# Four matmuls with a combined query weight in place of six, in the cached-key scores of the sample group

## The chip, the cores and the metric

The kernel runs on one core of one Trainium2 chip. A core has five engines that run their own instruction queues in order: PE (TensorE, matrix products into PSUM banks), DVE (VectorE), ACT (ScalarE), POOL (GpSimd) and SP (SyncE, which here issues most DMA transfers). They wait for each other through semaphores only. The time of a kernel is the device time of one execution in microseconds (us), given as the median of several runs. Beside the times there is one profiled execution, whose records (busy time of each engine, waits, the chain of work that ended last, the clock granted to PE) are quoted below.

## What is computed

The program is one step of a decoder layer for two groups of tokens that share all weights: a prompt of 1024 tokens and a sample group of 8 sequences with 8 new tokens each (64 tokens, in all 1088 columns). A layer has two token mixers side by side (sparse attention with an indexer that picks 256 keys per query, and gated linear attention), an output projection, a layer norm, a squared-ReLU MLP with 4096 hidden channels and a second layer norm.

The change is in the sparse attention of the sample group. For each of the 8 sequences, 8 queries by 8 heads (64 rows) are compared with 4096 keys of a paged cache and with the new keys; keys that were not picked are masked; softmax and the product with the values follow. Cut to that:

```python
s = jnp.einsum('bqkgd,bqskd->bqkgs', qg, k_sel).astype(jnp.float32) * (HEAD_DIM ** -0.5)
s = jnp.where(valid[:, :, None, None, :], s, -jnp.inf)
p = jax.nn.softmax(s, axis=-1).astype(v_sel.dtype)
o = jnp.einsum('bqkgs,bqskd->bqkgd', p, v_sel)
```

The kernel doesn't gather the picked keys: it scores all 4096 cached keys and adds a mask of large negative numbers.

Every fp32 number that enters a matmul is split into a high part (rounded to the type `fp32r`) and a low part (the remainder). A product x·y is then formed as three matmuls: high·high, high·low and low·high, which add up in one PSUM bank.

## The kernel before, in words

The program has two parts. `front` makes all projections, the indexer, the prompt's attention and the gated linear attention; it is not touched, and its instructions are the same in both kernels. `back` holds the MLP, and inside it, as work that is dealt in between, the sample group's attention on its cache.

**Who sets the order.** The program is unrolled when it is built. A planner (`Clock`, `Stream`, `Order`) holds a list of Python generators, the streams. Each yields what its next step needs, as tiles that must be ready or as a condition. The planner keeps an estimated time for each engine (`Clock.note`, fed by `Clock.cost`), and always takes the first stream of the list whose needs are met by the time of PE; `slack` says by how much DVE and ACT may be booked ahead of PE and the stream still be stepped. So the order of each engine's queue is fixed when the program is built. On the chip each engine takes its queue in that order.

**The filler.** `main` (through `feed`, `ff1_unit`, `ff2_unit`) is the MLP for column blocks 0 and 1 (384 columns each), in groups of four hidden blocks. One unit of the first layer is 24 matmuls of 384 columns into a bank named `pf1`, one of the second is 12 matmuls into `pf2` (the profile calls both `pf`). It is the last stream in the list and is stepped whenever nothing else may be. A unit's result goes through ACT and DVE (`fr`), ACT (`a`) and DVE or POOL (the low part of `a`).

**The scores.** `at_scores` works on four pairs of sequences p, eight chunks of 512 keys each. A chunk n is loaded by eight DMAs on SP (`k_load`, tile `ckr`), split by ACT (`ckh`, high) and DVE or POOL (`ckl`, low) in `k_split`, and multiplied with the queries `aqz` into a bank `psc`. The queries of a pair lie as the 128 columns of a weight: 64 columns for sequence 0 of the pair, 64 for sequence 1. There are four such weights in `aqz`, of 128 columns each: for either sequence the high part and the low part, with zeros in the other sequence's 64 columns, so that both sequences' scores add up in one bank (rows 0 to 63 and 64 to 127):

```python
pe.matmul(ps[:, :n], qz[:, b2, 0], kh, start=first, stop=False)
pe.matmul(ps[:, :n], qz[:, b2, 0], kl, start=False, stop=False)
pe.matmul(ps[:, :n], qz[:, b2, 1], kh, start=False, stop=b2 == 1)
```

One DVE instruction then adds the mask (`msk`, `asn` for the new keys), writes the scores to SBUF (`as`, `ast` for the new keys) and keeps the row's maximum (`amx`). At the start of each pair `at_scores` loads `aq`, clears `aqz` on POOL and fills it by eight small casts on DVE. There is one `aqz`.

**The values.** `at_values` transposes the weights of the softmax (`pst`, `ptl`), multiplies them with the cached values (`cv`, banks `pob`), and at a pair's end divides, transposes back (`sa`, `pso`) and collects (`tall`).

**The merge.** `merge` waits for all four pairs, then multiplies the sample group's columns (block 2, 320 columns) with the attention output weights (`pma`, eight weights `wao`) and the output projection (`pwo`, eight weights `wout`). Its weights come through `Weights V`: raw tiles `vr` (tag `rw`, six buffers, shared with the MLP's raw weights `wr`), split into `v`. After its layer norm the MLP for block 2 runs to the end, followed by the last layer norm.

Of the kernel before, what the change touches and what calls it, by code (L numbers as in the profile page):

```python
# [12 lines left out]
F32 = mybir.dt.float32  # L13
F32R = mybir.dt.float32r
# [3 lines left out]
AF = mybir.ActivationFunctionType  # L18
# [5 lines left out]
P = 128  # L24
# [67 lines left out]
def f32(ap):  # L92
    return ap.bitcast(F32)
# [1902 lines left out]
def back(ph, tc, env, A, O):  # L1996
# [20 lines left out]
    def own(name, shape, dt=F32, bufs=1):  # L2017
        return clock.take(pgs.tile(shape, dt, name=name, tag=name, bufs=bufs), name, "own " + name, bufs)
# [20 lines left out]
    class Weights:  # L2039
# [10 lines left out]
        def load(self):  # L2050
            i = self.split + len(self.raw)
            src, kt = self.src[i]
            rs = []
            if self is W and 3 <= i < 6:
                r = wide(f"{self.name}r{i}", F32, [P, 8, P])[:, :kt]
                sp.dma_start(r, src)
                rs = [r[:, k:k + 4] for k in range(0, kt, 4)]
            for k in range(0, 0 if rs else kt, 4):
                r = clock.take(pgs.tile([P, 4, P], F32, name=f"{self.name}r{i}_{k}", tag="rw", bufs=NRW), f"{self.name}r{i}_{k}", "brw", NRW)
# [316 lines left out]

    def at_scores():
# [6 lines left out]
        for p in range(4):  # L2384

            aq = own("aq", [P, 8, 16], F32R)
            sp.dma_start(f32(aq), f32(env["qa_s"][:, :, TP + 16 * p:TP + 16 * p + 16].rearrange("h p q -> p h q")))
            qz = own("aqz", [P, 512], F32R)
            q6 = qz.rearrange("p (b e c h q) -> p b e c h q", b=2, e=2, c=2, h=8)
            qz = qz.rearrange("p (b e x) -> p b e x", b=2, e=2)  # L2390
            pool.memset(f32(qz), 0.0)
            yield [aq]
            for g in range(2):
                for e in range(2):
                    for par in range(2):
                        r = ((par + e) % 2) * 64
                        x = q6[g * 64:g * 64 + 64, 0, e, 0, 4 * g + par:4 * g + par + 3:2, :]
                        x = view(x, 0, [x.ap[0], [256 + 64, 2], x.ap[1], x.ap[2]])
                        dve.tensor_copy(x, f32(aq[r:r + 64, 4 * g + par:4 * g + par + 3:2]).rearrange("p h (b q) -> p b h q", b=2))
                yield ()  # L2400
# [7 lines left out]
            def scores(ps, n, kb, k0, mcol):  # L2408
                first = True
                for b2 in range(2):  # L2410
                    kh, kl = kb[b2]
                    if n == 512:
                        kh, kl = (x.rearrange("p (i j r) -> p j i r", i=4, j=4) for x in (kh, kl))
# [3 lines left out]
                    first = False  # L2417
                i = k0 // 1024
                so, si = S[i][:, k0 - 1024 * i:k0 - 1024 * i + n], ps[:, :n]
                m = mn if n < 512 else mks[4 * p + i][:, k0 - 1024 * i:k0 - 1024 * i + n]  # L2420
                dve.tensor_tensor_reduce(out=so, in0=si, in1=m, scale=1.0, scalar=NEG, op0=OP.add, op1=OP.max,
                                         accum_out=mx[:, mcol:mcol + 1])
            for qq in range(4):
                yield lambda: len(used) >= 4 * (p - 1) + qq
                S[qq] = xpage(f"as{p}{qq}", F32, [P, 1024])
                for e in range(2):
# [7 lines left out]
                    ps = bank("psc")  # L2434
                    scores(ps, 512, [(h[:, b2], l[:, b2]) for b2 in range(2)], qq * 1024 + e * 512, qq * 2 + e)
# [3 lines left out]
            ps = bank("psc")  # L2439
            scores(ps, TS, [(ka_n[:, 0], ka_n[:, 1])] * 2, PAST, 8)  # L2440
# [11 lines left out]
            blocks.append(S)  # L2452

# [78 lines left out]
    def merge():  # L2532
        yield lambda: "samples" in flags
# [7 lines left out]
        V.load(), V.load()  # L2541
# [13 lines left out]
        for f in range(8):  # L2555
            yield V.landed(1 if f else 2)
            w = V.get(f, 1, 1)
# [11 lines left out]
        yield from outputs(2, lambda f: V.get(8 + f, 1, 2), wide)  # L2569
# [150 lines left out]
    order.add(at_values(), margin=M_VA)  # L2720
    order.add(at_scores(), margin=M_SC)
# [84 lines left out]
```

## Time and profile before

| | before |
|---|---|
| time, median of 3 runs | 2037.97 us (2036.68 to 2038.39) |
| the profiled execution, its own time | 2039.02 us |
| its span, first to last instruction | 2037.3 us |
| mean clock granted to PE | 0.996 of full speed |
| PE, matmuls busy | 2012.7 us, 99% |
| DVE, ACT, POOL busy | 60%, 55%, 38% |
| first and last matmul of the scores (`psc`) | 1190.6 and 1486.2 us |
| matmuls of the merge (`pma`, `pwo`) | 1610.7 to 1717.7 us |

All numbers below are of the span's clock: 0 is the first instruction of the profiled execution. A row of the view of groups names the engine, the operation, the output tile, the input tiles, the shapes, the count, the busy time and the mean duration of one. All instructions have the line L263, since a helper records them; they are told apart by their tiles. The durations that the profile gives for single matmuls overlap each other, so the cost of a matmul to PE is read from a run of them (start of the first to start of the next work) divided by their number.

### The profile page before, as it was taken

How to read it: one execution, taken by the hardware profiler on the slowest of the kernel's cores; microseconds unless marked ns; L12 is line 12 of the kernel's file. 1: busy time of each engine (PE TensorE's matmuls, PEld its weight loads, DVE VectorE, ACT ScalarE, POOL GpSimd, SP SyncE). 2: the span in 40 equal slices, each digit the busy share in tenths (PEclk: the TensorE clock that was granted, in tenths of full speed). 3: DMA queues.
4: the chain of work that ended last, by engine and by line, in shares of the span. 5: the costliest groups of instructions: out<-in, count | busy, mean ns of one | idle time of the engine just before them, and what ended most of it. 6: DMA issues, size and time to landing. Idle time of an engine off the chain costs nothing.

```text
span 2037.3 us, 34522 instructions
## 1 busy us (share of the span) xinstructions
PE 2012.7 (99%) x12439; PEld 1949.4 (96%) x12439; DVE 1227.1 (60%) x2597; ACT 1114.6 (55%) x2217; POOL 775.4 (38%) x582
## 2 busy tenths in 40 slices
PE   9999999999999999999999999999999999999998
PEld 8999999999999999999999999998999999999998
DVE  8897767785655866641366445566554445466635
ACT  6687788897778566650124344544443232445543
POOL 5144232232311131222133335565654343354455
PEclk9999999999999999999999999999999999999998
DMA  9465212212132342364661245554523443145552
GB/s 329 182 211 155 99 35 71 80 54 85 41 115 71 95 144 71 100 221 141 216 222 52 65 121 167 163 166 136 156 90 103 141 132 100 52 141 163 185 151 91
DMA packets 185164, 260.32 MB, mean 128 GB/s; under 512 B 22160, under 2 KB 121488, under 8 KB 184992
## 3 DMA queue, kind: packets, MB, share of 16 engines
q1 hardware_dynamic: 177440, 232.67, 36.0%
q0 software_dynamic: 7552, 25.43, 4.2%
q8 instruction: 98, 1.61, 0.3%
q14 instruction: 74, 0.61, 0.1%
HBM read 208.52 MB, written 49.51 MB: 127 GB/s over the span
## 4 chain that ended last, share of the span: by engine, by line
PE 53%; issue 2%; ACT 1%; DVE 1%; POOL 1%; SPq 0%; DMA 0%; ACTq 0%; POOLq 0%; DVEq 0%
PE pf L263 34%; PE pwo L263 5%; PE pmb L263 4%; PE gate L263 2%; PE pma L263 2%; PE psc L263 2%; PE pob L263 1%; PE pst L263 1%; SPq L263 0%; PE pov L263 0%; ACT pp L263 0%; PE ppt L263 0%; POOL w L263 0%; POOL wl L263 0%; ACT as L263 0%
## 5 line engine op out<-in xcount | busy, mean ns | idle before, releaser
L263 PE MATMUL pf<-a,w 128*128 128x384 f32 (+1 forms) x2304 | 398.3, 330 | 1.5 <-POOL a L263 0.6
L263 PE MATMUL pf<-h,w 128*128 128x384 f32 (+1 forms) x2304 | 394.3, 329 | 0.0
L263 PEld LDWEIGHTS pf<-a,w 128*128 128x128 f32 x2304 | 379.6, 188 | 5.4 <-POOL a L263 0.9
L263 PEld LDWEIGHTS pf<-h,w 128*128 128x128 f32 x2304 | 380.2, 188 | 1.9
L263 POOL TENSOR_TENSOR wl<-wr,wh 128x1024 fp32r<-128x1024 f32 (+1 forms) x67 | 152.9, 2287 | 420.4 <-ACT wh L263 324.7
L263 POOL TENSOR_TENSOR w<-wr,w 128x512 fp32r<-128x512 f32 x135 | 191.1, 1423 | 124.9 <-ACT w L263 114.5
L263 ACT ACTIVATE w<-wr 128x512 fp32r<-128x512 f32 x256 | 147.6, 618 | 39.0 <-PE pf L263 25.9
L263 DVE TENSOR_TENSOR w<-wr,w 128x512 fp32r<-128x512 f32 x121 | 126.8, 1053 | 55.8 <-ACT w L263 54.4
L263 DVE TENSOR_TENSOR acc<-acc,pf 128x384 f32<-128x384 f32 (+1 forms) x152 | 81.4, 539 | 104.9 <-PE pf L263 104.7
L263 POOL TENSOR_TENSOR a<-fr,a 128x384 fp32r<-128x384 f32 (+1 forms) x56 | 54.6, 976 | 199.5 <-ACT a L263 197.1
L263 PE MATMUL gate<-xh,wh 128*128 128x384 f32 (+1 forms) x384 | 129.0, 336 | 0.0
L263 PE MATMUL gate<-xh,wl 128*128 128x384 f32 (+1 forms) x384 | 125.7, 327 | 0.0
L263 PE MATMUL gate<-xl,wh 128*128 128x384 f32 (+1 forms) x384 | 125.6, 327 | 0.0
L263 ACT ACTIVATE wh<-wr 128x1024 fp32r<-128x1024 f32 (+1 forms) x76 | 75.3, 998 | 85.3 <-PE pmb L263 65.9
L263 ACT ACTIVATE fr<-pf 128x384 f32<-128x384 f32 (+1 forms) x96 | 44.9, 467 | 122.9 <-PE pf L263 122.0
L263 DVE TENSOR_TENSOR fr<-fr,pf 128x384 f32<-128x384 f32 (+1 forms) x96 | 50.8, 529 | 95.2 <-ACT fr L263 94.8
L263 ACT ACTIVATE a<-fr 128x384 fp32r<-128x384 f32 (+1 forms) x96 | 48.7, 508 | 77.5 <-DVE fr L263 77.5
L263 DVE TENSOR_SCALAR_CACHE_REDUCE jk<-sc,ga_f 128x1024 int8<-128x1024 f32 (+2 forms) x96 | 88.2, 919 | 1.7
L263 ACT ACTIVATE jkb<-sc,gb_f 128x896 int8<-128x896 f32 (+2 forms) x96 | 86.1, 897 | 5.6 <-DVE gb_f L263 3.2
L263 PE MATMUL psv<-wh,xh 128*128 128x256 f32 x288 | 80.8, 285 | 0.0
L263 PE MATMUL psv<-wl,xh 128*128 128x256 f32 x288 | 80.4, 283 | 0.0
L263 DVE CUSTOM_DVE_ANT_0 pp<-psq,msk 128x512 f32<-128x512 f32 (+3 forms) x96 | 51.4, 554 | 46.2 <-PE psq L263 44.1
(525 smaller groups left out, 5149.9 us busy)
## 6 DMA issues: line engine op xcount, KB each, us to landing
wr<-wff SPq DMA_DIRECT2D x254, 256.0 KB
wr<-w SPq DMA_DIRECT2D x42, 512.0 KB
ckr<-kT SPq DMA_DIRECT2D x256, 64.0 KB
ga_s<-gate SPq DMA_DIRECT2D x16, 544.0 KB
ci_s<-cig SPq DMA_DIRECT2D x16, 512.0 KB
kir<-ci_s SPq DMA_DIRECT2D x16, 512.0 KB
mgp<-ga_s SPq DMA_DIRECT2D x16, 384.0 KB
qa_s<-qa SPq DMA_DIRECT2D x8, 544.0 KB
```

The source lines that it names most:

```text
L263: r = f(*a, **k)
```

## The change

The queries' high part and low part now lie side by side in one weight of 128 columns, one weight for each sequence of a pair: 64 columns high, 64 columns low (for the second sequence the other way round). Each of the two parts of the keys is multiplied with it, into a bank of its own for each sequence. So a chunk takes four matmuls instead of six, and half of a bank holds the scores from the high part of the queries, the other half those from the low part (with low·low, which was left out before). The halves are added afterwards: ACT copies one half (64 rows) to SBUF, DVE adds the other half from PSUM, and the instruction with mask and maximum then reads and writes SBUF. This tail is a stream of its own (`fin`), placed first in the planner's list.

The queries are made by a stream of their own, `at_queries`, with two buffers of `aqz` (256 columns each), from the beginning of the pair before. The streams `at_values` and `at_scores` get `slack=8.0` instead of 2.0. The raw weights of the merge (`Weights V`) are taken into the three buffers of `msk` where one is free in the planner's count, the first two are loaded once the scores are done (flag `scored`), and more raw tiles may be held (3 and 4 instead of 1 and 2).

```diff
-                                  ("aq", [P, 8, 16], F32R, 1), ("aqz", [P, 512], F32R, 1), ("ast", [P, TS], F32, 2), ("amx", [P, 9], F32, 2),
+                                  ("aq", [P, 8, 16], F32R, 1), ("aqz", [P, 256], F32R, 2), ("ast", [P, TS], F32, 2), ("amx", [P, 9], F32, 2),
...
+                if self is V and clock.free.get("own msk", [0]):
+                    r = clock.take(pgs.tile([P, 4, P], F32, name=f"{self.name}r{i}_{k}", tag="msk", bufs=3), f"{self.name}r{i}_{k}", "own msk", 3)
+                else:
+                    r = clock.take(pgs.tile([P, 4, P], F32, name=f"{self.name}r{i}_{k}", tag="rw", bufs=NRW), f"{self.name}r{i}_{k}", "brw", NRW)
...
+    def at_queries():
+        yield lambda: "start" in flags
+        for p in range(4):
+            yield lambda: pair[0] >= p - 1
+            aq = own("aq", [P, 8, 16], F32R)
+            sp.dma_start(f32(aq), f32(env["qa_s"][:, :, TP + 16 * p:TP + 16 * p + 16].rearrange("h p q -> p h q")))
+            t = own("aqz", [P, 256], F32R, bufs=2)
+            pool.memset(f32(t), 0.0)
+            qz = t.rearrange("p (b x) -> p b x", b=2)
+            q5 = t.rearrange("p (c h q) -> p c h q", c=4, h=8)
+            yield [aq]
+            for g in range(2):
+                for e in range(2):
+                    for par in range(2):
+                        r = ((par + e) % 2) * 64
+                        x = q5[g * 64:g * 64 + 64, e, 4 * g + par:4 * g + par + 3:2, :]
+                        x = view(x, 0, [x.ap[0], [64 if e else 192, 2], x.ap[1], x.ap[2]])
+                        dve.tensor_copy(x, f32(aq[r:r + 64, 4 * g + par:4 * g + par + 3:2]).rearrange("p h (b q) -> p b h q", b=2))
+                yield ()
+            qzs[p] = qz
...
-                    pe.matmul(ps[:, :n], qz[:, b2, 0], kh, start=first, stop=False)
-                    pe.matmul(ps[:, :n], qz[:, b2, 0], kl, start=False, stop=False)
-                    pe.matmul(ps[:, :n], qz[:, b2, 1], kh, start=False, stop=b2 == 1)
...
+                ps = [bank(f"psc{b2}", True) for b2 in range(2)]
                 for b2 in range(2):
+                    for e in range(2):
+                        k = kb[b2][e]
...
+                        pe.matmul(ps[b2][:, :n], qz[:, b2], k, start=e == 0, stop=e == 1)
...
-                dve.tensor_tensor_reduce(out=so, in0=si, in1=m, scale=1.0, scalar=NEG, op0=OP.add, op1=OP.max,
-                                         accum_out=mx[:, mcol:mcol + 1])
+                def fin():
+                    for b2 in range(2):
+                        yield [ps[b2][:, :n]]
+                        act.activation(so[64 * b2:64 * b2 + 64], ps[b2][64 - 64 * b2:128 - 64 * b2, :n], AF.Copy)
+                    for b2 in range(2):
+                        x = so[64 * b2:64 * b2 + 64]
+                        yield [x]
+                        dve.tensor_tensor(x, ps[b2][64 * b2:64 * b2 + 64, :n], x, op=OP.add)
+                        unpin(ps[b2])
+                    dve.tensor_tensor_reduce(out=so, in0=so, in1=m, scale=1.0, scalar=NEG, op0=OP.add, op1=OP.max,
+                                             accum_out=mx[:, mcol:mcol + 1])
+                    summed.append(0)
+                order.add(fin(), engines=(), at=0)
...
     def merge():
+        yield lambda: "scored" in flags
+        V.load(), V.load()
         yield lambda: "samples" in flags
...
-        V.load(), V.load()
...
-            w = V.get(f, 1, 1)
+            w = V.get(f, 1, 3)
...
-        yield from outputs(2, lambda f: V.get(8 + f, 1, 2), wide)
+        yield from outputs(2, lambda f: V.get(8 + f, 1, 4), wide)
...
-    order.add(at_values(), margin=M_VA)
-    order.add(at_scores(), margin=M_SC)
+    order.add(at_values(), margin=M_VA, slack=8.0)
+    order.add(at_queries(), margin=M_SC)
+    order.add(at_scores(), margin=M_SC, slack=8.0)
```

The planner lays out the whole of `back` anew, so the queues differ from the first score on. On PE the first chunk (the first `psc` of the program; `ckh` and `ckl` are the keys' two parts) stands before as

```order
L263 MATMUL psc<-ckh_12990,aqz 128x512
L263 MATMUL psc<-ckl_12991,aqz 128x512
L263 MATMUL psc<-ckh_12990,aqz 128x512 x2
L263 MATMUL psc<-ckl_12991,aqz 128x512
L263 MATMUL psc<-ckh_12990,aqz 128x512
```

and now as

```order
L263 MATMUL psc_12991<-ckh_12926,aqz 128x512
L263 MATMUL psc_12991<-ckl_12927,aqz 128x512
L263 MATMUL psc_12992<-ckh_12926,aqz 128x512
L263 MATMUL psc_12992<-ckl_12927,aqz 128x512
```

Six matmuls into one bank have become four into two banks. It also stands 48 matmuls of `pf` earlier in PE's queue, and the last chunk stands later: 1470 matmuls of `pf` lie ahead of the end of the fourth pair's scores in the new stage, counted from its first chunk; before, 1176.

On DVE, the place where the fourth pair's queries are filled (the casts `aqz<-aq`) stands before between the end of the third pair's softmax (`asm`, `rcs`) and the third pair's output (`sa`), just ahead of the fourth pair's first chunk:

```order
L263 TENSOR_TENSOR acc_12157<-acc_12157,pf_15786 128x384
L263 TENSOR_REDUCE asm<-asm 128x1
L263 RECIPROCAL asm<-asm 128x1
L263 COPY rcs<-asm 64x1 x2
L263 CAST aqz<-aq 64x2x2x8 x8
L263 TENSOR_TENSOR acc_12473<-acc_12473,pf_15800 128x384
L263 TENSOR_TENSOR w_0_15873<-wr_0_15531,w_0_15873 128x512
L263 TENSOR_TENSOR sa_15885<-pob_14882,sa_15885 64x256
```

Now the same eight casts stand within the tail of the third pair's first chunks (`as` is their score page), a whole pair ahead of their use:

```order
L263 TENSOR_TENSOR w_1_15174<-wr_4_14935,w_1_15174 128x512
L263 TENSOR_TENSOR as_15017<-psc_15116,as_15017 64x512
L263 CAST aqz<-aq 64x2x2x8 x8
L263 TENSOR_TENSOR fr<-fr,pf_15181 128x384
L263 TENSOR_TENSOR as_15017<-psc_15209,as_15017 64x512
L263 TENSOR_TENSOR as_15017<-psc_15117,as_15017 64x512
L263 ISA as_15017,amx<-as_15017,msk 128x512
L263 ISA amx 128x1
```

The casts have left the boundary between two pairs; the rows with a `psc` and 64x512 are the new additions of the halves, and the row `ISA as,amx<-as,msk` is the mask and maximum, which now reads SBUF.

On SP, the DMA queue of the merge, the raw weights of the output projection (`vr<-wout`) stand before as

```order
L263 DMA vr_0_18406<-wout 128x512
L263 DMA vr_4_18408<-wout 128x512
L263 DMA wr_0_18452<-wff 128x512
L263 DMA z_18479<-xT 128x2x320
L263 DMA z_18481<-xT 128x2x320
L263 DMA vr_0_18483<-wout 128x512
L263 DMA vr_4_18485<-wout 128x512
L263 DMA vr_0_18493<-wout 128x512
L263 DMA vr_4_18495<-wout 128x512
```

with MLP weights among them to the end, and the middle of them stands now as

```order
L263 DMA vr_0_18867<-wout 128x512
L263 DMA vr_4_18869<-wout 128x512
L263 DMA vr_0_18871<-wout 128x512
L263 DMA vr_4_18873<-wout 128x512
L263 DMA vr_0_18938<-wout 128x512
L263 DMA vr_4_18940<-wout 128x512
L263 DMA z_18969<-xT 128x2x320
L263 DMA vr_0_18977<-wout 128x512
L263 DMA vr_4_18979<-wout 128x512
```

Three weights are asked for in a row where two were, and the `pwo` matmuls on PE stand closer: by weights (24 matmuls each) they come as one, two, three and two, with 24, 12 and 18 matmuls of `pf` in between; before, 12 to 36 matmuls of `pf` stood within or around each single weight, up to the last two.

More of the change, by code (lines that the diff above doesn't have):

```diff
@@ L2375, in v_load @@
         vraw[n] = r
+    qzs, pair, summed = {}, [-1], []
+    def at_queries():
[18 more added lines that the diff above has]
+            qzs[p] = qz
     def at_scores():
@@ L2384, in at_scores @@
         for p in range(4):
[L2386 to L2400, printed above, removed]
+            yield lambda: p in qzs
+            qz = qzs.pop(p)
+            pair[0] = p
+            yield [qz]
             S = [None] * 4 + [own("ast", [P, TS], bufs=2)]
@@ L2406, in at_scores, with scores @@
                 sp.dma_start(mn[64 * b2:64 * b2 + 64], view(env["mk_s"], (64 + 16 * p + 8 * b2) * 2 * T + HALF, [[0, 8], [2 * T, 8], [1, TS]]))
-            def scores(ps, n, kb, k0, mcol):
-                first = True
+            def scores(n, kb, k0, mcol):
+                ps = [bank(f"psc{b2}", True) for b2 in range(2)]
                 for b2 in range(2):
-                    kh, kl = kb[b2]
-                    if n == 512:
-                        kh, kl = (x.rearrange("p (i j r) -> p j i r", i=4, j=4) for x in (kh, kl))
-                    pe.matmul(ps[:, :n], qz[:, b2, 0], kh, start=first, stop=False)
-                    pe.matmul(ps[:, :n], qz[:, b2, 0], kl, start=False, stop=False)
-                    pe.matmul(ps[:, :n], qz[:, b2, 1], kh, start=False, stop=b2 == 1)
-                    first = False
+                    for e in range(2):
+                        k = kb[b2][e]
+                        if n == 512:
+                            k = k.rearrange("p (i j r) -> p j i r", i=4, j=4)
+                        pe.matmul(ps[b2][:, :n], qz[:, b2], k, start=e == 0, stop=e == 1)
                 i = k0 // 1024
-                so, si = S[i][:, k0 - 1024 * i:k0 - 1024 * i + n], ps[:, :n]
+                so = S[i][:, k0 - 1024 * i:k0 - 1024 * i + n]
                 m = mn if n < 512 else mks[4 * p + i][:, k0 - 1024 * i:k0 - 1024 * i + n]
-                dve.tensor_tensor_reduce(out=so, in0=si, in1=m, scale=1.0, scalar=NEG, op0=OP.add, op1=OP.max,
-                                         accum_out=mx[:, mcol:mcol + 1])
+                def fin():
[11 more added lines that the diff above has]
+                order.add(fin(), engines=(), at=0)
             for qq in range(4):
@@ L2433, in at_scores @@
                     yield [h, l, mks[4 * p + qq]]
-                    ps = bank("psc")
-                    scores(ps, 512, [(h[:, b2], l[:, b2]) for b2 in range(2)], qq * 1024 + e * 512, qq * 2 + e)
+                    scores(512, [(h[:, b2], l[:, b2]) for b2 in range(2)], qq * 1024 + e * 512, qq * 2 + e)
             for n in range(p * 8, p * 8 + VAHEAD):
@@ L2438, in at_scores @@
             yield ()
-            ps = bank("psc")
-            scores(ps, TS, [(ka_n[:, 0], ka_n[:, 1])] * 2, PAST, 8)
+            scores(TS, [(ka_n[:, 0], ka_n[:, 1])] * 2, PAST, 8)
+            yield lambda: len(summed) == 9 * p + 9
             dve.tensor_reduce(sm[:, 0:1], mx, axis=AX.X, op=OP.max)
@@ L2452, in at_scores @@
             blocks.append(S)
+        flags.add("scored")
     def at_values():
```

1 line of the change is left out of this document (removed).

## The prediction

> **What bounds the kernel now.** I read the page's busy times first, then the windows by stage, then what PE waited for, then the timeline at PE's two longest pauses in the stage of the scores.
>
> ```profile
> PE 2012.7 (99%) x12439; PEld 1949.4 (96%) x12439; DVE 1227.1 (60%) x2597; ACT 1114.6 (55%) x2217; POOL 775.4 (38%) x582
> ```
>
> PE is without matmul for 24.6 us of 2037.3 (2037.3 - 2012.7). Over so long a span an average can hide a stage with another limit, so the windows (columns: PE, PEld, DVE, ACT, POOL busy with counts, granted clock, share of the DMA engines, GB/s):
>
> ```profile
> 1200.00:1300.00 100.00, 100.00 (x576) 96.27 (x575) 55.70 (x97) 46.27 (x77) 55.18 (x41) 1.00 0.56 162
> 1300.00:1400.00 100.00, 98.88 (x584) 94.26 (x583) 62.02 (x112) 50.69 (x90) 58.47 (x47) 1.00 0.57 160
> 1400.00:1500.00 100.00, 96.93 (x558) 92.32 (x557) 53.67 (x96) 46.08 (x85) 59.57 (x47) 0.97 0.42 126
> 1600.00:1700.00 100.00, 100.00 (x608) 100.00 (x607) 44.22 (x67) 31.29 (x59) 40.00 (x34) 1.00 0.45 144
> ```
>
> The first three hold nearly all scores (1190 to 1486 us), the fourth most of the merge. PE is full in all of them, DVE and ACT have 38 to 54 of 100 us free. What is taken from PE here is taken from the end, as long as the MLP's filler lasts and nothing new makes PE wait.
>
> **What the change takes from PE.** Three rows of the chain of waits (start, duration, work):
>
> ```profile
> 1211.08 1.40 PE psc L263 x6
> 1212.48 5.24 PE pf L263 x30
> 1231.01 2.00 PE psc L263 x12
> ```
>
> A chunk's six matmuls of 512 columns take 1.40 us, 0.234 each (other chunks show 1.41). There are 32 chunks and each loses two: 64 x 0.234 = 15.0 us. The row of twelve is one chunk and the six matmuls on the 64 new keys, so these cost (2.00 - 1.40) / 6 = 0.10 us each; four pairs lose two each: 8 x 0.10 = 0.8 us. Sum **15.8 us**. All of it lies on PE, beside nothing. A filler matmul costs 5.24 / 30 = 0.175 us and their number stays.
>
> **What goes with the queries' place.** PE's waits and the two pauses:
>
> ```profile
> PE psc L263 <- DVE aqz L263: 2.5, 1, 2.5
> PE psc L263 <- DVE ckl L263: 1.0, 1, 1.0
> ```
>
> (us in total, times, longest), and the windows of 10 us around them:
>
> ```profile
> 1320.00:1330.00 10.00, 8.88 (x46) 7.55 (x45) 8.25 (x17) 3.93 (x7) 8.26 (x6) 1.00 0.09 23
> 1410.00:1420.00 10.00, 6.93 (x27) 5.64 (x27) 9.75 (x20) 1.26 (x2) 7.01 (x6) 0.79 0.47 139
> 1420.00:1430.00 10.00, 10.00 (x54) 9.04 (x53) 3.69 (x10) 2.16 (x4) 4.59 (x5) 0.87 0.29 77
> 1430.00:1440.00 10.00, 10.00 (x63) 9.63 (x62) 4.86 (x8) 5.00 (x8) 4.86 (x4) 1.00 0.41 119
> ```
>
> Both pauses stand at the boundary of two pairs, before the first chunk of the third and of the fourth. The timeline of the later one:
>
> ```profile
> 1406.63 4.89 POOL L263 TENSOR_TENSOR ckl<-ckr,ckh 128x1024 fp32r<-128x1024 f32 x2
> 1407.81 6.66 DVE L263 CAST aqz<-aq 64x32 fp32r<-64x32 f32 x8
> 1414.34 0.47 PE L263 MATMUL psc<-ckh,aqz 128*128 128x512 f32 x1 [2.45 <-DVE aqz L263]
> 1416.67 0.36 PE L263 MATMUL pso<-idf,sa 64*128 64x64 f32 x1 [0.62 <-DVE sa L263]
> 1416.96 2.29 PE L263 MATMUL pf<-a,w 128*128 128x384 f32 x6
> ```
>
> The eight casts lie on DVE while POOL subtracts, take 6.66 us instead of some 1.4 (median 0.176 each, row below), and PE stands until the last is done; then it waits for `sa`, which lay behind the casts. Afterwards its clock is granted at 0.79 and 0.87: six matmuls of `pf` take 2.29 us where thirty take 5.24. The price: idle 1.12 + 3.07 = 4.2 us (10 minus busy), and for the clock 0.21 x 6.93 + 0.13 x 10 = 2.8 us; together 7.0 us. (Counting matmuls against the 63 of the next full window gives more: 17 + 36 + 9 = 62 missing, at 0.16 us about 10 us; they are of several sizes, so I keep 7.0.) In the new order the casts stand a pair ahead and `aqz` has two buffers, so PE no longer stands behind them.
>
> The Trainium skill, "TensorE: Matmul & The Clock Gate", Part 1, has a clock that is halved after an idle window of about 3.4 us and comes back after as long of work. By it one pause would cost an estimated 1.7 us of clock, and the gain here would be 5.9 instead of 7.0. The rows agree in kind: 3.07 us idle brought the clock down, 1.12 us did not.
>
> **What the change adds.** All of it is on DVE and ACT:
>
> ```profile
> L263 DVE CUSTOM_DVE_ANT_0 as<-psc,msk x32: 673/692/693, 1192.2 to 1485.9; 128x512 f32<-128x512 f32 x32
> L263 DVE CAST aqz<-aq x32: 170/176/2393, 1185.5 to 1414.3; 64x32 fp32r<-64x32 f32 x32
> L263 ACT ACTIVATE sa<-pob x8: 369/376/382, 1320.6 to 1586.1; 64x256 f32<-64x256 f32 x8
> L263 DVE TENSOR_TENSOR sa<-pob,sa x8: 405/408/416, 1327.6 to 1588.4; 64x256 f32<-64x256 f32 x8
> L263 DVE TENSOR_TENSOR ptl<-pst,ptl 128x512 fp32r<-128x512 f32 x32 | 22.0, 688 | 24.3 <-ACT ptl L263 24.3
> L263 ACT ACTIVATE ptl<-pst 128x512 fp32r<-128x512 f32 x32 | 19.0, 592 | 72.2 <-PE pst L263 72.2
> L263 DVE TENSOR_TENSOR v<-vr,v x10: 679/711/1799, 1616.8 to 1710.9; 128x512 fp32r<-128x512 f32 x10
> ```
>
> The duration goes by columns, not rows: 64x256 takes DVE 0.408 us, 128x512 from PSUM 0.688. So an addition of two halves (64x512) is taken at 0.69 us, a copy on ACT at 0.59. Two of each in 32 chunks: DVE 64 x 0.69 = 44 us, ACT 64 x 0.59 = 38 us; the eight small ones of either engine, bounded above by the 64x256 rows, add at most 3.3 and 3.0. The mask with maximum read PSUM and mask at an even 0.69 us and now reads SBUF twice: no row has that. The nearest with two SBUF inputs of 512 columns goes from 0.68 to 1.80 us, so 36 of them add 0 to 40 us; I take 5, near that row's median of 0.71. The casts stay 32 in number, and the clearing of `aqz` on POOL gets shorter.
>
> DVE was busy for 55.70 + 62.02 + 53.67 = 171 us of these 300, so with 44 + 3 + 5 it has 223, 74%; ACT has 143 + 41 = 184, 61%. In PE's new queue the stage is longer, too: 1470 matmuls of the filler to the end of the scores where 1176 were, 294 x 0.175 = 51 us more of filler beside the same scores. So the additions are hidden, and cost PE nothing as long as no single one is waited for. Queued behind a tail's copy on ACT are `fr` and `a` of the MLP; `a` of a group's last unit is what PE needs next. In the new queue the tightest such place leaves PE about 4.6 us of other work, and the path `fr`, `fr`, `a`, low part takes some 0.5 + 0.55 + 0.53 + 1.0 us by this profile's means, with one tail's copies or one key split (1.05 to 1.3 us) in front. That is close, so I allow 3.5 us of new pauses: between 0 (the scores' pauses gone and none back) and 7.0 (as much lost in other places), halfway.
>
> The filler lasts: behind the sample group's layer norm PE's queue keeps 204 filler matmuls (36 us) where it had 306 (53 us). SP gets the same transfers; the first two raw weights of the merge go out earlier, past MLP weights, at a time when the DMA engines are busy for 0.42 to 0.57 of their time.
>
> **The sum.** 2037.3 - 15.8 - 7.0 + 3.5 = 2018.0 us of span. The span lies 0.7 us under the median (2037.97; the profiled execution took 2039.02), so the median should be **2018.7 us**, 0.9% less. Own range of this case: 2012 (no new pause, 10 instead of 7.0 given back) to 2024 (new pauses of 9 instead of 3.5).
>
> **Rivals.**
>
> *New pauses on the MLP's path.* The tails go first in the planner's list and the streams may be booked 8 us ahead on ACT and DVE, so `fr` and `a` come later at the group boundaries. For it: the 4.6 us above. Against: DVE and ACT at 74 and 61%. Some five groups at 2 us each, the clock once (2.8 us): 13 us of loss in place of 3.5, 2028 us. Faster still.
>
> *DVE held up by POOL.* If each of the 36 maxima takes 1.80 us, DVE gets 35 us more than I took, 258 of 300 us, 86%. Then the tails end late, the two banks of a chunk stay taken, and PE waits at nearly every chunk; at 1 us a chunk the sum is 2018.7 - 3.5 + 32 = 2047, **slower**. It decides from about 0.7 us a chunk on (22.8 / 32, the way from 2015.2 to 2038). For it: the casts of 1407.81, held up beside POOL's subtraction (maximum 2.39 us). Against: DVE's own subtraction of that form has its median at 0.71, and nothing on PE reads the maximum before the pair's end. The Trainium skill, "SBUF — State Buffer", section "Who interferes with whom", says that a DVE instruction with two SBUF inputs contends with a GpSimd instruction that reads SBUF, one with at most one SBUF input doesn't; the new maximum changes from the second kind to the first. The rows of 693 and 1799 ns maximum agree.
>
> *The merge starves.* Its output projection now comes in up to three weights in a row:
>
> ```profile
> 1694.50 4.19 PE pf L263 x24
> 1698.70 3.51 PE pwo L263 x24
> 1683.93 0.88 SPq L263 DMA_DIRECT2D vr<-wout  x2
> 1686.84 1.29 ACT L263 ACTIVATE v<-vr 128x512 fp32r<-128x512 f32 x2 [6.25 <-DMA vr<-wout]
> L263 POOL TENSOR_TENSOR v<-vr,v x14: 1299/1307/1760, 1599.2 to 1710.4; 128x512 fp32r<-128x512 f32 x14
> ```
>
> PE eats a weight in 3.51 us; from issue to landing are 2.9 us (1683.93 to 1686.84), then 1.29 on ACT and 1.3 for the low part, 5.5 in all. If each weight were asked for only when the last is split, PE would lose 2.0 us on each of eight, 16 us: 2034.7. ACT already waits 6.25 us for such a transfer. Against: up to two weights are asked for ahead, which covers 7.0 us.
>
> *No effect.* If PE's full rows were stretched by waits the removed matmuls would leave gaps: 2038. Against: the even 1.40 us.
>
> **How the numbers follow.** My forecast 0.68; pauses on the MLP's path 0.17; starved merge 0.05; DVE held up 0.06; no effect 0.04. About 0.2% (4 us) is what can be told from no change. Faster: 0.68 + 0.17 and a little of the merge, 0.86; within 0.2%: no effect and the rest of the merge, 0.08; slower 0.06. For 8 in 10 the range is 2011 to 2030: it takes in the first rival, and leaves out the merge, DVE and no effect, 0.15, and a little below the low end, which I put 1 us under the own range's.
>
> **What would show it.** Right: 128 and 16 matmuls of `psc` at 0.234 and 0.10 us; no wait of `psc` for `aqz`, and granted clock 1.00 in the windows of the scores; additions near 0.69 us; DVE under 80% there. Wrong: `psc` waiting for banks or `ckl` at many chunks (DVE), `pf` waiting for `a` (MLP), `pwo` waiting for `v` (merge), or a gain over 26 us, which would need pauses outside this stage to go.

## The result and the profile after

The changed kernel takes **2021.3 us** (median of 4 runs, 2020.31 to 2023.08), the kernel before 2037.54 (median of 4, 2036.68 to 2038.39). The ratio is 0.9921, with an interval of 0.9904 to 0.9938: 16.2 us less. The forecast was 2018.7, the range 2011 to 2030. The profiled execution took 2022.21 us, its span is 2020.5.

First the page's busy times, then the windows of the same stretches as before (PE, PEld, DVE, ACT, POOL busy with counts, granted clock, share of the DMA engines, GB/s):

```profile
PE 1997.2 (99%) x12367; PEld 1936.2 (96%) x12367; DVE 1279.1 (63%) x2677; ACT 1153.2 (57%) x2289; POOL 775.5 (38%) x574
```

```profile
1200.00:1300.00 100.00, 99.10 (x572) 96.45 (x571) 76.42 (x119) 57.77 (x101) 50.42 (x34) 1.00 0.52 148
1300.00:1400.00 100.00, 99.08 (x584) 95.24 (x584) 73.38 (x131) 58.11 (x104) 61.05 (x47) 1.00 0.54 155
1400.00:1500.00 100.00, 100.00 (x597) 97.22 (x597) 70.98 (x121) 56.36 (x101) 58.88 (x46) 1.00 0.50 153
1600.00:1700.00 100.00, 100.00 (x605) 98.96 (x604) 44.79 (x78) 33.09 (x64) 40.99 (x36) 1.00 0.46 144
```

PE is busy for 15.5 us less with 72 matmuls less, and still 99% of the span. In the stage of the scores DVE stands at 71 to 76% where it was at 54 to 62, ACT at 56 to 58. The granted clock is 1.00 in all of them; the wait of `psc` for `aqz` is gone. What is new is small pauses of PE: in the first two windows 0.90 and 0.92 us are missing. In the timeline of PE (start, duration, work, in brackets the idle time before it and who ended it) three of them read:

```profile
1296.34 1.03 PE L263 MATMUL pf<-a,w 128*128 128x384 f32 x2 [0.76 <-ACT a L263]
...
1327.63 0.66 PE L263 MATMUL pst<-idf,as 128*128 128x128 f32 x4 [0.74 <-DVE acc L263]
...
1519.19 1.07 PE L263 MATMUL pob<-cv,ptl 128*128 128x256 f32 x7 [0.74 <-DVE ptl L263]
```

What the tails cost on DVE and ACT, by groups of the stretch 1180 to 1540 us (busy time, mean ns of one, idle time before it and what ended it):

```profile
L263 DVE TENSOR_TENSOR as<-psc,as 64x512 f32<-64x512 f32 x64 | 43.9, 686 | 3.8 <-ACT as L263 2.7
L263 DVE CUSTOM_DVE_ANT_0 as<-as,msk 128x512 f32<-128x512 f32 x32 | 33.9, 1059 | 1.1
L263 ACT ACTIVATE as<-psc 64x512 f32<-64x512 f32 x64 | 38.0, 593 | 45.8 <-PE psc L263 44.8
```

Additions and copies came out as priced (0.69 and 0.59 us). The maximum, with two SBUF inputs, has a mean of 1.06 us. The timeline ahead of the pause at 1296.34 shows one of the long ones:

```profile
1292.19 2.40 POOL L263 TENSOR_TENSOR ckl<-ckr,ckh 128x1024 fp32r<-128x1024 f32 x1 [0.68 <-ACT ckh L263]
1292.52 2.62 DVE L263 CUSTOM_DVE_ANT_0 as<-as,msk 128x512 f32<-128x512 f32 x1
...
1295.18 0.56 DVE L263 TENSOR_TENSOR fr<-fr,pf 128x384 f32<-128x384 f32 x1
1295.77 0.52 ACT L263 ACTIVATE a<-fr 128x384 fp32r<-128x384 f32 x1 [3.28 <-DVE fr L263]
```

The maximum starts 0.33 us into a subtraction of POOL and lasts until after it; `fr` stands behind it on DVE, ACT waits 3.28 us for `fr`, and PE waits for `a`. It suggests a theory for the new pauses, *held maximum*, which the first runs test.

### The profile page after: what moved, and what is told of

Same layout as the page of the kernel before. It is cut to its first block, busy times and chain, and to the rows that moved or that the text cites. A ratio compares the mean times of both kernels' runs of the same rounds, so it can differ in the third digit from the quotient of the medians.

```text
span 2020.5 us, 34501 instructions
## 1 busy us (share of the span) xinstructions
PE 1997.2 (99%) x12367; PEld 1936.2 (96%) x12367; DVE 1279.1 (63%) x2677; ACT 1153.2 (57%) x2289; POOL 775.5 (38%) x574
## 4 chain that ended last, share of the span: by engine, by line
PE 47%; issue 4%; DVE 3%; ACT 2%; POOL 2%; DMA 1%; SPq 0%; ACTq 0%; POOLq 0%; DVEq 0%
PE pf L263 30%; PE pwo L263 5%; PE pmb L263 4%; PE pma L263 2%; PE gate L263 2%; PE pob L263 1%; PE psc L263 1%; DVE as L263 1%; POOL w L263 1%; PE pst L263 0%; DVE fr L263 0%; DMA obl<-ob_s 0%; POOL a L263 0%; SPq L263 0%; ACT as L263 0%
```

## The experiments

In most of these kernels an instruction was added or left out behind the planner's back: the planner books the old work, so that all queues but the named one keep their order. "Same plan" stands for that; PE's queue is then that of the kernel it was made from, but for the instructions named. In the others the planner set the queues anew, and the text says so. Differences are of medians; the kernel before had 2037.3 to 2037.8 in each session, and the changed kernel's 2021.3 is that of its four runs above, which lie 2.8 us apart. So differences under 2 us are not read from medians. In the cuts of code `half b2`, `own half` and `other half` stand for ranges of 64 rows, and calls that only tell the planner of work are left out.

### The price of the tail

```
-                        act.activation(so[half b2], ps[b2][other half], AF.Copy)
...
-                        dve.tensor_tensor(x, ps[b2][own half], x, op=OP.add)
...
-                    dve.tensor_tensor_reduce(out=so, in0=so, in1=m, ...)
+                    nc.vector.tensor_tensor_reduce(out=so, in0=ps[1][:, :n], in1=m, ...)
```

> Edit of the changed kernel: the copies of the halves and the two additions are left out, and the maximum reads one bank of PSUM with the mask (so half of each score is missing from the output). PE's queue is instruction for instruction that of the changed kernel; DVE has 72 instructions fewer, ACT 72. It prices all that the tail costs PE. Theory 'tail' (the six new pauses of the changed kernel, 3.8 us of idle PE and its restarts, come from the work that was added on DVE and ACT): they go, 2021.3 - 6 = 2015 to 2016 us, and no pf, pst or pob waits in 1290 to 1520. Rival 'order' (they come from PE's new queue and the transfers, whatever DVE and ACT do): 2020 to 2022 us, with the pauses at the same matmuls.

Measured: 2017.78 us (2017.28 to 2018.24), 3.5 less than the changed kernel; spans 2020.5 and 2016.5. The stretch 1180 to 1540 of this kernel, and of the changed one:

```profile
1180.00:1540.00 360.00, 359.89 (x2111) 349.30 (x2110) 200.57 (x372) 168.16 (x299) 191.56 (x147) 1.00 0.48 145
```

```profile
1180.00:1540.00 360.00, 357.38 (x2085) 345.46 (x2084) 258.99 (x442) 205.60 (x368) 197.16 (x147) 1.00 0.49 144
```

With PE's queue the same, 2.5 us of its 2.6 us of idle time are gone. The pauses come from the tail, not from PE's new order. The whole price of 58 us more on DVE (259.0 for 200.6) and 37 us more on ACT (205.6 for 168.2) is 3.5 us.

### Is it the held maximum?

Three kernels share this question. In the first the maximum is issued twice (the mask is then added twice, too):

```
                     dve.tensor_tensor_reduce(out=so, in0=so, in1=m, ...)
+                    nc.vector.tensor_tensor_reduce(out=so, in0=so, in1=m, ...)
```

> Edit of the changed kernel: each maximum over the scores with the mask (two SBUF inputs, mean 1.06 us) is issued twice, outside the planner's sight, so that PE's and ACT's queues stay as they are. DVE gets 32 x 1.06 + 4 x 0.41 = 36 us more in 300, from 68 to about 76%. Theory 'held maximum' (the pauses come where a maximum beside POOL's subtractions is stretched to 2.6 or 3.6 us): the chances double, some 6 us of pauses more, 2027 us, and single maxima up to 3.5 us ahead of the new waits. Rival 'no price' (DVE's load is far from deciding): 2021 to 2023 us. Rival 'DVE is the bound' (the slower rival of the prediction): over 2035 us.

In the second the tail needs no copies and no instruction with two SBUF inputs:

```
-                        act.activation(so[half b2], ps[b2][other half], AF.Copy)
...
-                        dve.tensor_tensor(x, ps[b2][own half], x, op=OP.add)
+                        nc.vector.tensor_tensor(x, ps[b2][other half], m[half b2], op=OP.add)
+                        nc.vector.tensor_tensor_reduce(out=x, in0=ps[b2][own half], in1=x, op0=OP.add, op1=OP.max, ...)
...
-                    dve.tensor_tensor_reduce(out=so, in0=so, in1=m, ...)
```

> Edit of the changed kernel: no copies on ACT; for each half DVE adds the mask to the other bank's half (PSUM + SBUF to SBUF) and then takes sum and maximum of its own bank's half with that (PSUM + SBUF). Four DVE instructions of 64x512 per chunk, an estimated 4 x 0.69 = 2.76 us against 2 x 0.69 + 1.06 = 2.43 now, none with two SBUF inputs; ACT has 38 us less. PE's queue is that of the changed kernel. Theory 'held maximum': the pauses go, 2015 to 2017 us, though DVE has some 10 us more. Rival 'DVE load': the pauses stay or grow, 2021 to 2023 us.

The third is the second with the copies still on ACT:

```
+                        act.activation(so[half b2], ps[b2][other half], AF.Copy)
```

> As the kernel of the tail from PSUM, but ACT still copies the halves (its results are overwritten by DVE, which waits for them as in the changed kernel): PE's and ACT's queues are those of the changed kernel, only DVE's maximum with two SBUF inputs is gone, for 0.3 us more of DVE per chunk. Theory 'held maximum': as without the copies, 2015 to 2017 us. Rival 'ACT' (the copies in ACT's queue ahead of fr and a make the pauses): 2020 to 2023 us, while the run without copies is at 2015 to 2017.

Measured: maximum twice 2039.78 us (2037.39 to 2042.58), **18.5 more** than the changed kernel and no faster than the kernel before. Tail from PSUM 2020.76 (2020.21 to 2021.85), by its median not to be told from the changed kernel. With the copies 2027.33 (2026.13 to 2027.9), 6.6 more than without them and 6.0 more than the changed kernel.

The theory that held maxima make the pauses falls as it stands: in the third kernel every instruction of the tail is even, and it is slower than the changed one. Its DVE rows:

```profile
L2442 DVE TENSOR_TENSOR as<-psc,msk 64x512 f32<-64x512 f32 x64 | 44.1, 689 | 5.0 <-ACT as L263 3.1
L2443 DVE CUSTOM_DVE_ANT_0 as<-psc,as 64x512 f32<-64x512 f32 x64 | 44.1, 689 | 2.2
L263 DVE TENSOR_TENSOR ckl<-ckr,ckh 128x1024 fp32r<-128x1024 f32 x22 | 27.8, 1262 | 26.4 <-ACT ckh L263 20.4 <-DMA ckr<-kT 4.3 <-issue 1.6
```

An even 0.689 us throughout, 88.2 us for the tail where the changed kernel has 77.8 (43.9 + 33.9): **10.4 us more of even work cost 6.0 us**. Doubling the maximum added 26.7 us (31.1 + 29.5 - 33.9) and the short reading of its result, and cost 18.5:

```profile
L263 DVE CUSTOM_DVE_ANT_0 as<-as,msk 128x512 f32<-128x512 f32 x32 | 31.1, 972 | 1.1
L2445 DVE CUSTOM_DVE_ANT_0 as<-as,msk 128x512 f32<-128x512 f32 x32 | 29.5, 923 | 1.1
```

So with the copies in place the price grows with the work on DVE, also where none of it is held. The 18.5 us are in the range of the rival "DVE is the bound", but DVE is busy for 273 of the 360 us there, 76%; what PE loses is 10.8 us more of idle time in the stage (346.6 busy for 357.4), and a granted clock of 0.98 over it where it was 1.00.

That the copies matter shows in the second kernel, which has the same 88 us of tail on DVE and none on ACT, and is 6.6 us faster than the third. The waits suggest the way. DVE's longest wait in the changed kernel (view of waits: total, times, longest):

```profile
DVE ckl L263 <- ACT ckh L263: 21.8, 12, 4.2
```

With copies, ACT stands 44.8 us in 20 waits for `psc`, and key splits (`ckh`) lie behind these copies in its queue; DVE then idles 21.8 us for `ckh` and does its tails in bursts. Without copies that wait of DVE is 2.1 us, by the row of its groups (second kernel):

```profile
L263 DVE TENSOR_TENSOR ckl<-ckr,ckh 128x1024 fp32r<-128x1024 f32 x22 | 27.7, 1258 | 9.1 <-DMA ckr<-kT 5.1 <-ACT ckh L263 2.1 <-DMA wr<-wff 1.8
```

How much of the 3.5 us the stretched maximum has by itself, no run separates: the second kernel takes away the held maxima and the copies together and adds 10 us of even work. In its profiled execution PE idles 0.8 us in the stage (359.2 of 360 busy) where the changed kernel has 2.6, so some of the price may be gone there; four runs each can't tell that from chance. In the kernel with the maximum twice PE waits where the MLP's and the values' streams come late, as the prediction's first rival had it, and not at the chunks:

```profile
PE pob L263 <- DVE ptl L263: 5.0, 5, 2.1
PE pf L263 <- ACT a L263: 4.9, 2, 3.0
PE pf L263 <- DVE w L263: 1.9, 1, 1.9
```

### The matmuls and the queries by themselves

```
+                        if e == 0:
+                            nc.tensor.matmul(ps[b2][:, :n], qz[:, b2], k, start=True, stop=True)
                         pe.matmul(ps[b2][:, :n], qz[:, b2], k, start=e == 0, stop=e == 1)
```

> Edit of the changed kernel: the first matmul of either bank is issued twice (the second overwrites the first), outside the planner's sight, so that all queues but PE's stay as they are and PE has its 64 matmuls of 512 columns and 8 of 64 again. It prices the main term by itself. Theory 'PE is the bound': 64 x 0.234 + 8 x 0.10 = 15.8 us more, 2037 us. Rival 'cover': with more matmuls beside the same DVE and ACT work the tail's pauses close, which gives back up to the 3.5 us that leaving out the tail gave, 2033 to 2034 us.

Measured: 2036.63 us (2035.73 to 2038.87), 15.3 more; the profiled spans differ by 14.1, and PE's busy time by 14.9 (1997.2 and this row of the page):

```profile
PE 2012.1 (99%) x12439; PEld 1948.3 (96%) x12439; DVE 1282.1 (63%) x2677; ACT 1154.3 (57%) x2289; POOL 777.8 (38%) x574
```

PE's idle time over the whole span (span minus busy) is 22.5 us where it was 23.3. So PE is the bound, the matmuls cost nearly what they were priced at, and of the 3.5 us that the rival had at most 1 or 2 come back under the longer scores.

The kernel before without the casts of three pairs' queries:

```
-                        dve.tensor_copy(x, y)
+                        if p == 0:
+                            dve.tensor_copy(x, y)
+                        else:
+                            clock.note("dve", "tensor_copy", (x, y), {})
```

> Edit of the kernel before: the casts of the queries of pairs two to four are left out (their scores are then those of zero queries), the planner still counts them, so that PE's and ACT's queues are those of the kernel before. It prices the two pauses behind the casts by themselves. By the prediction's term: 7.0 us less, 2030.5 us. By what is left between the spans of before, the changed kernel without a tail and 15.8 us of matmuls: 5.0 us less, 2032.5 us. Rival 'something else is late next' (sa and ckl lie beside the casts): 1 to 3 us less, 2034.5 to 2036.5 us.

Measured: 2032.33 us (2031.25 to 2033.55), ratio 0.9972 (0.9962 to 0.9982): **5.2 us less**, 3.7 to 7.7 by the interval. In its stretch PE is full:

```profile
1180.00:1540.00 360.00, 360.00 (x2108) 346.74 (x2107) 198.97 (x346) 168.26 (x297) 208.40 (x164) 1.00 0.50 147
```

The 4.2 us in which PE idled in this stretch of the kernel before (355.8 of 360 busy) are gone, so the casts were the whole cause of the two pauses; nothing else was late behind them.

What the lower clock has in this can be read from a third kernel, the one before with the early loads of the merge (below): its queue on PE is the same until after the scores, and its profiled execution has the same pause at the same place, but with the clock at full speed (the fourth pair's first score, the MLP's six matmuls and the two windows to compare with those at 0.79 and 0.87):

```profile
1414.33 0.48 PE L263 MATMUL psc<-ckh,aqz 128*128 128x512 f32 x1 [2.45 <-DVE aqz L263]
1416.87 1.32 PE L263 MATMUL pf<-a,w 128*128 128x384 f32 x6
...
1410.00:1420.00 10.00, 6.87 (x33) 5.25 (x32) 9.75 (x20) 1.26 (x2) 7.01 (x6) 1.00 0.48 141
1420.00:1430.00 10.00, 10.00 (x64) 9.96 (x63) 4.13 (x11) 3.08 (x6) 4.60 (x5) 1.00 0.36 111
```

The rows of the scores in the three kernels (before, with the early loads, without casts) give the length of the stage, first to last start:

```profile
L263 PE MATMUL psc<-ckh,aqz x128: 392/397/629, 1190.6 to 1485.4; 128*128 128x512 f32 x128
L263 PE MATMUL psc<-ckh,aqz x128: 394/397/483, 1190.4 to 1482.9; 128*128 128x512 f32 x128
L263 PE MATMUL psc<-ckh,aqz x128: 395/396/483, 1192.2 to 1479.7; 128*128 128x512 f32 x128
```

That is 294.8, 292.5 and 287.5 us: 5.0 us for the pauses and 2.3 for the clock where it falls. It fell in the profiled execution of the kernel before, whose mean clock is 0.996. Of the 57 executions of that kernel that were timed beside the experiments, 48 have 0.997 or 0.998, and 9 have 0.995 or 0.996, so the median holds little or nothing of it.

The changed kernel with the casts back at their pair's start:

```
+            for x, y in casts[p]:
+                nc.vector.tensor_copy(x, y)
             yield [qz]
```

> Edit of the changed kernel: the eight casts of a pair's queries are issued on DVE at the pair's own start, as before the change, and no more a pair ahead; PE's and ACT's queues are those of the changed kernel. It prices the queries' place by itself. By the prediction's term (idle and lower clock of two pauses): 7.0 us more, 2028 us. By what the run without the tail leaves (span 2037.3 before - 15.8 for the matmuls - 2016.5 without the tail): 5.0 us more, 2026 us. Rival 'order' (the two pauses belonged to the old queue of PE): 2020 to 2023 us.

Measured: 2022.94 us (2019.95 to 2024.34), against 2021.3 (2020.31 to 2023.08): no difference that can be told, and none of the four runs reaches the 2026 or 2028 us expected. Four runs alone would not shut out 5 us, but the profile does: `psc` has no wait for `aqz`, and the first to the last start of `psc<-ckh` takes 324.7 us (1180.7 to 1505.4) where the changed kernel has 324.9 (1182.2 to 1507.1). The start of the fourth pair in its timeline:

```profile
1427.78 5.48 PE L263 MATMUL pf<-h,w 128*128 128x384 f32 x30
1427.84 2.63 POOL L263 TENSOR_TENSOR ckl<-ckr,ckh 128x1024 fp32r<-128x1024 f32 x1 [0.18 <-DMA ckr<-kT]
...
1428.83 2.79 DVE L2417 CAST aqz<-aq 64x32 fp32r<-64x32 f32 x8
...
1433.39 0.50 PE L263 MATMUL psc<-ckh,aqz 128*128 128x512 f32 x1
```

The casts are held again (2.79 us beside POOL's subtraction), but PE has thirty matmuls of filler beside them and needs them 1.8 us after they end (1.4 and 1.6 us at the second and third pair). The pair's start is reached earlier there on DVE than on PE. That the casts stand a pair ahead is therefore not what gives the 5 us in this order; that they are done before PE comes is. What makes that room in the new order was not tried by itself.

### The other parts of the change

```
-    order.add(at_values(), margin=M_VA, slack=8.0)
+    order.add(at_values(), margin=M_VA)
...
-    order.add(at_scores(), margin=M_SC, slack=8.0)
+    order.add(at_scores(), margin=M_SC)
```

> Edit of the changed kernel: the streams of scores and values may be booked 2 us ahead on ACT and DVE, as before the change, instead of 8; all queues are planned anew. If the wider slack is what makes the tails stand ahead of the MLP's instructions: the tail's pauses shrink, 2018 to 2020 us. If it is what lets casts, key splits and tails be done before PE comes to them: pauses at psc and pob as in the kernel before, 2025 to 2035 us.

Measured: 2035.32 us (2033.78 to 2039.21), **14 us more** than the changed kernel. What PE waited for up to 1770 us, and a window behind the merge:

```profile
PE pf L263 <- DVE ptl L263: 2.0, 1, 2.0
PE pob L263 <- DVE asm L263: 1.4, 1, 1.4
PE pf L263 <- ACT a L263: 1.2, 2, 1.0
...
1780.00:1800.00 20.00, 15.99 (x79) 14.36 (x78) 18.19 (x30) 10.29 (x22) 8.25 (x7) 0.83 0.24 81
```

The size is that of the second theory, the place is not: `psc` waits for nothing even so; the pauses are at the values and the MLP. The merge is late as well (its last `pwo` starts at 1750.4 us, in the changed kernel at 1718.1), and behind it the filler ends before the sample group's layer norm. Since all queues are new, the 14 us price the order that the planner finds with 2 us of slack; they are not the price of the slack by itself.

```
-        yield lambda: "scored" in flags
-        V.load(), V.load()
         yield lambda: "samples" in flags
...
+        V.load(), V.load()
...
-            w = V.get(f, 1, 3)
+            w = V.get(f, 1, 1)
```

> Edit of the changed kernel: the output projection's raw weights are loaded where they were before the change (behind the last group, in their own buffers, one and two weights ahead). It prices that part of the change. Theory 'covered' (the MLP's filler lasts through the merge, PE is full there): 2021 to 2022 us. Rival 'starved': pwo waits for v, up to 2 us at each of eight weights, 2025 to 2037 us. A gain would show in 1590 to 1760 us alone: none there now, 2020 us at best.

Measured: 2029.74 us (2029.26 to 2030.47), **8.4 more**. The queues are planned anew from the merge on. The merge's own stretch stays full, but the last matmul of the output projection starts at 1747.7 us, where it was 1718.1, and PE is held up behind it (the tile's row, waits and windows of this kernel):

```profile
L263 PE MATMUL pwo<-mg,v x192: 302/309/312, 1681.1 to 1747.7; 128*128 128x320 f32 x192
...
PE plm L263 <- POOL ls L263: 2.3, 1, 2.3
...
1760.00:1780.00 20.00, 17.67 (x99) 16.75 (x98) 13.65 (x23) 6.53 (x13) 13.02 (x11) 0.94 0.23 73
1780.00:1800.00 20.00, 18.40 (x107) 17.32 (x106) 15.79 (x28) 11.52 (x24) 8.02 (x7) 0.89 0.30 99
```

The starved merge does not make `pwo` wait, since PE fills the time with the MLP; it pushes the end of the projection, and with it the samples' layer norm, back by 30 us, past the end of that filler at 1775 us.

The kernel before with this part alone:

```
+        yield lambda: "scored" in flags
+        V.load(), V.load()
         yield lambda: "samples" in flags
...
-            w = V.get(f, 1, 1)
+            w = V.get(f, 1, 3)
```

> Edit of the kernel before: only the part of the change on the merge (first two raw weights of the output projection in the masks' buffers behind the last scores, three and four of them ahead). In the changed kernel undoing this part cost 8.4 us, since the sample group's layer norm ended some 30 us later and the MLP's filler ran out at 1776 us. Theory 'filler' (the part is worth something only where the filler ends before the samples' layer norm; before has 53 us of it behind the norm): no change, 2036 to 2039 us, with the merge's last pwo earlier than 1718 us. Rival 'the part gains by itself': 2029 to 2034 us.

Measured: 2037.8 us (2036.12 to 2038.5), ratio 1.0001 (0.9991 to 1.001): nothing that can be told (2 us either way by the interval), though its projection ends 18 us earlier (1699.5 for 1717.7):

```profile
L263 PE MATMUL pwo<-mg,v x192: 302/309/312, 1664.2 to 1699.5; 128*128 128x320 f32 x192
```

So this part is worth nothing alone and 8.4 us in the changed kernel, where less filler is left. This is what the theory "filler" had foretold.

### A tail from PSUM that the planner knows

The edit is that of the tail from PSUM, with all calls visible to the planner.

> Edit of the changed kernel: the tail from PSUM on DVE alone (four instructions of 64x512 with one PSUM and one SBUF input, no copies on ACT), now known to the planner, which sets all queues anew. With the old plan it took 2020.8 us with one pause of 0.5 and one of 0.2 us left. Theory 'the plan can close the rest': 2017 to 2019 us. Rival 'a new order brings its own pauses': 2020 to 2024 us.

Measured: 2040.39 us (2038.82 to 2042.95), **19.6 more** than the same work in the changed kernel's order. Its timeline at the start of the third pair:

```profile
1331.69 2.44 POOL L263 TENSOR_TENSOR ckl<-ckr,ckh 128x1024 fp32r<-128x1024 f32 x1
1332.51 8.22 DVE L263 CAST aqz<-aq 64x32 fp32r<-64x32 f32 x8
1334.43 2.40 POOL L263 TENSOR_TENSOR ckl<-ckr,ckh 128x1024 fp32r<-128x1024 f32 x1 [0.31 <-ACT ckh L263]
1341.95 0.34 PE L263 MATMUL pso<-idf,sa 64*128 64x64 f32 x1 [4.91 <-DVE sa L263]
1342.21 2.29 PE L263 MATMUL pf<-a,w 128*128 128x384 f32 x6
```

It is the old pause in a new place: the casts are held for 8.22 us beside POOL, `sa` stands behind them on DVE, PE waits 4.91 us for it, and then six matmuls take 2.29 us at a granted clock of 0.50 (window 1342 to 1344). Neither the expected gain nor the rival's size was right. No version was found that is measurably faster than the changed kernel; with PE's queue as it is, leaving the tail out altogether would give 3.5 us.

## Why the prediction was nearly right

**The matmuls** (15.8 us): right. Put back by themselves they cost 14.1 (spans) to 15.3 us (medians), and the counts foretold, 128 and 16 matmuls of `psc`, are there.

**The old pauses** (7.0 us): right in mechanism, too large by the clock. The run without casts gives 5.2, and what is left between the spans of before, the kernel without a tail and the 15.8 us is 5.0. The prediction took 4.2 us of idle time and 2.8 of lower clock from one profiled execution, at 2039.02 us slower than the median. Both are there in that execution (5.0 and 2.3 by the rows of the scores); but the same pause in the kernel with the early loads left the clock at 1.00, and by their mean clock most executions had no such loss. So the idle time belongs into a forecast of the median and most of the clock's share does not. The estimate of 5.9 by the Trainium skill, "TensorE: Matmul & The Clock Gate", Part 1, counts one loss of clock in every execution too; that it lies nearer to 5.2 is no evidence for its 1.7 us.

**That the casts' new place is what gives this back:** wrong, as the step was put. With the casts at their old place in the changed queues PE did not wait for them; the new order alone leaves them 1.4 to 1.8 us of room. The slack of 8 us, which the prediction counted only as a danger (tails ahead of `fr` and `a`), is part of what makes that order: planned with 2 us instead, the kernel takes 14 us more, with pauses at `ptl`, `asm` and `a`, and a late merge. Which part of the change makes the room for the casts stays open.

**The new pauses** (3.5 us, allowed halfway between two ends): 3.5 measured. The size was no reckoning, only the middle between 0 and 7.0, so that it came out to the tenth is luck. The place was the one named, the paths of `fr` and `a`, and beside it `acc` and `ptl`; the 13 us of the rival that had such pauses at every group did not come. The chunk's maximum was put at 5 us more in all and takes 11.8 more (33.9 for 32 x 0.69); the stage could still bear that. The additions and copies and the 74% for DVE (71 to 76) came as worked out; ACT has 56 to 58% for 61.

**The rival "DVE held up"** (2047 us): it did not come, and in its direction it had some truth. It asked what 35 us more in the maxima than the 27 reckoned would do; with the maximum twice they take 60.6 us, 33.5 more than reckoned, and the kernel 2039.8 us, slower than before as the rival had it, if by less. Its way was another, though: PE waited for `ptl`, `a` and `w`, and nowhere for a bank of `psc`.

**The rival "starved merge"**: the late loads do cost 8.4 us, by another path than the one worked out (not `pwo` waiting for `v`, but the samples' layer norm outlasting the filler). The change's early loads prevent it, and the statement that 36 us of filler are left holds only with them. The prediction gave them no worth.

**The sum**, from the runs: 15.3 for the matmuls, 5.2 for the pauses, less 3.5 for the tail, is 17.0; 16.2 were measured. The forecast's 19.3 was too much by the 1.8 us of the pauses, 0.5 of the matmuls, and 0.8; the last two are within what the runs can tell.

## What to carry to other kernels

Where one engine is full and others carry queues in order, price a change to the full engine by the work removed, and price what is added elsewhere by a run that holds the plan and leaves the added work out: 58 us on DVE, with 37 on ACT, cost 3.5 here; from there 10 us more on DVE cost 6.0, and 27 us more cost 18.5. A new plan for the same work moved this kernel by 14 to 20 us, about what the removed matmuls save, so an experiment that lets the planner run again tests the order first and the edit second. A part that gives nothing alone (the early loads, 1.0001) can be what keeps another part's gain (8.4 us): the cover that a cost of nothing rests on is used up by the gain itself. And a loss of clock behind a pause that one profile shows is to be held against the mean clock of the other executions before it goes into a forecast of the median.

## What the runs showed of the hardware

**Casts beside POOL.** Eight casts of 64x32 take 1.28 us where POOL doesn't subtract (changed kernel, at 1355.75) and 2.79, 6.66 and 8.22 beside POOL's subtractions, though they have one SBUF input. The Trainium skill, "SBUF — State Buffer", section "Who interferes with whom", names casts among the instructions that can take the port pair shared with GpSimd; the rows agree. The longest single cast, 2.39 us in the kernel before, is as long as one of POOL's subtractions of 128x1024 (2.40 us). The new maximum with its two SBUF inputs takes 0.69 to 3.55 us. In the changed kernel's trace all 15 maxima over 0.8 us overlap a subtraction of POOL, and of the 17 shorter ones one does; of the 64 additions, with one input from PSUM and one from SBUF, 35 overlap one and stay even all the same (rows of the tile `as`). That fits the same section of the Trainium skill, by which two SBUF inputs contend with a GpSimd instruction that reads SBUF and at most one doesn't:

```profile
L263 DVE TENSOR_TENSOR as<-psc,as x64: 672/690/695, 1187.4 to 1512.1; 64x512 f32<-64x512 f32 x64
L263 DVE CUSTOM_DVE_ANT_0 as<-as,msk x32: 691/695/3546, 1190.9 to 1512.8; 128x512 f32<-128x512 f32 x32
```

**The clock after a short pause.** Windows of 2 us of the kernel before, around its longer pause:

```profile
1414.00:1416.00 2.00, 1.66 (x6) 1.05 (x6) 1.93 (x7) 0.20 (x1) 0.00 (x0) 0.95 0.62 174
1416.00:1418.00 2.00, 1.38 (x5) 1.21 (x5) 1.88 (x5) 0.42 (x1) 1.35 (x2) 0.50 0.51 172
1422.00:1424.00 2.00, 2.00 (x12) 1.96 (x12) 1.21 (x5) 1.01 (x2) 0.00 (x0) 0.84 0.04 16
```

PE stood for 2.45 us, until 1414.34, and for 0.62 us once more. The clock was halved not at once: 0.95 in the first window and 0.84 in the last put the half speed at about 1415.8 to 1422.6, some 1.5 us after PE had resumed and for 6.8 us. The same two pauses at the same places (2.45 and 0.68 us) in the profiled execution of the kernel with the early loads left the clock at 1.00, so the length of the pause alone does not decide it. The pauses of 0.74 and 0.76 us in the changed kernel left it at 1.00, too. The Trainium skill, "TensorE: Matmul & The Clock Gate", Part 1, puts the idle window at about 3.4 us; here a pause of 2.45 us, with the short one behind it, was enough in one execution and not in the other.
